# Layer-0 attention in bursts of six key tiles: maxima over two banks, the shift row put in by DMA, short units first, sums as products with a column of ones

## The chip, the cores and the metric

The kernel runs on one core of one Trainium2 chip, as one program. The metric is the device time of one execution in microseconds. Lower is better. The engines named below are PE (TensorE, matrix products; PEld is its weight load), DVE (VectorE), ACT (ScalarE), POOL (GpSimd) and SP (SyncE, which only issues DMAs here). They run at the same time, each through its own instructions in a fixed order, and wait for each other by semaphores.

## The reference

The reference is a two-layer backbone over 2048 latent tokens with a prefix of 256 context tokens, model width 1024, all in float32. Layer 0 runs a convolution branch beside grouped-query attention; layer 1 runs a Fourier branch beside neighbourhood attention. The change touches the attention of layer 0 alone. Cut to that:

```
ck = rms_norm(ck, kn_g)
q = axial_rope(rms_norm(q, qn_g))                 # 8 heads of 64
k = axial_rope(rms_norm(k, kn_g))                 # 2 key/value heads of 64
y_b = blocked_attn(q, concat([ck, k]), concat([cv, v]))   # 2304 keys
...
s = einsum('bqkgd,bskd->bkgqs', qg, k) * dh ** -0.5
p = softmax(s, axis=-1)
o = einsum('bkgqs,bskd->bqkgd', p, v)
...
yc_b = dense_attn(cq, ck, cv)                     # context queries: 256 keys
```

So 2048 latent queries of each of 8 heads see 2304 keys, and 256 context queries see the 256 context keys.

## The kernel before, in words

Tokens lie in 18 tiles of 128, the two context tiles first. A *unit* of the attention is 256 queries of two heads that share a key head: `(b, hp)`, with b the block of 256 tokens and hp the pair of heads. Its 4 x 128 = 512 query rows are the moving operand of the score products. A long unit (b from 1 to 8) goes over 18 key tiles, a short unit (b = 0, the context queries) over 2. There are 32 long and 4 short units; the short ones stand at places 0, 4, 8 and 12 of the list.

For each unit these functions run; all are closures in `ab_attention`:

- `load_q`, `load_high` (L866, L874): DMAs of the queries. A query is kept as a high and a low half in f32r; `q` holds both halves, `qm` the high half and further rows (see `shift_row`).
- `chunk` (L884, L886): maxima. The scores are computed once, roughly, with queries as stationary and 512 keys as moving operand into a PSUM bank of the pool `psm` (tile `m`, three buffers of one bank), and DVE reduces the bank to one column of `ast`. A long unit has 4 query tiles x 5 chunks, four of 512 keys and one of 256. The sign is turned, so the maximum is a minimum. `least` (L890) reduces the five columns to one.
- `shift_row` (L895, L896): the minima are transposed on PE into 4 rows, and DVE writes them, times a mask, into rows 64 to 67 of `qm`; the low half of the keys has four rows of ones there, so the second score product subtracts each query's shift.
- `score` (L907, L912): for one key tile two products into a bank of `pss` (tile `s`, two buffers), and ACT takes the exponential into `pr` (pool `apt`, six buffers).
- `multiply` (L922): for a pair of key tiles the value products, f32, 64 output columns each: the even tile into the upper half of the output partitions, the odd tile into the lower half, accumulated in one bank `av`. It stands three steps after the pair (LAG).
- `add` (L947): sums of the exponentials over key tiles; 11 of 18 tiles on POOL (`accp`), 7 on DVE (`accd`), two steps after the tile.
- `unload` (L930) copies `av` out on ACT. Then `join` (L952, POOL) adds the two sums, `sum_high` (L957, ACT) and `sum_low` (L962, DVE) split them into f32r halves, `total` (L972) multiplies a column of ones with both halves into one row, which ACT copies (L978) and a DMA spreads over 128 partitions (L980); `invert` (L986 to L989) takes the reciprocal, writes it to DRAM and reads it back broadcast to all partitions; `divide` (L993, POOL), `fold` (L998, L999, ACT) and `store` (L1005 to L1007) finish. The offsets of these eight are the tuple CHAIN.

The order of the work is written out by hand. A *step* is one key tile of one unit; `first[i]` is the step at which unit i starts. `at(step, order, f)` files a function under a step, and the loop at the end of `ab_attention` calls them by step and order, which fixes the order of instructions on PE, ACT, DVE and POOL (`manual_schedule`). Chunks of a unit are filed every 0.85 steps, the last of them 7 steps (AHEAD) before the unit's first score. SP's order isn't written out; the framework's scheduler places the DMAs. Beside the attention, `extra` runs side chains at given steps: adaLN products of the gate and of layer 1 (L238 and below), bias patterns for layer 1 (DMAs at L276 and near), and from step 220 on the first blocks of the layer's output stage.

## Time and profile before

| | us |
|---|---|
| three runs, lowest / median / highest | 2870.37 / 2875.66 / 2879.15 |
| the profiled execution, its own time | 2871.33 |
| its span, first to last instruction | 2869.4 |
| PE / weight loads busy | 2741.3 / 2107.3 |
| DVE / ACT / POOL busy | 1823.9 / 1117.7 / 1451.9 |
| value products `av`, PE busy | 315.5 |
| exponentials, ACT busy | 343.2 |
| first and last exponential of this attention, start | 705.1 and 1534.7 |

How to read it: times in the profile are microseconds from the start of the span, mean durations nanoseconds. A line of a group has the source line, the engine, the operation, the tiles as output<-input, the shapes, the number of instructions, and then the busy time with the mean of one, and the idle time of the engine just before them with what ended it. A line of the timeline has start, duration, engine, source line and the rest. Matmuls overlap: the end of one is modelled, and what one costs is the distance from its start to the start of the next. The granted clock is the share of TensorE's full clock.

### The profile page before, as it was taken

What the parts mean: (1) busy time and instruction counts of PE and PEld (TensorE: products, weight loads), DVE (VectorE), ACT (ScalarE), POOL (GpSimd) and SP (SyncE); (2) the same over time, 40 slices, a digit from 0 to 9 for tenths busy, and PEclk for the clock granted to TensorE, in tenths of its full rate; (3) what the DMA queues carried; (4) which work ended last, traced back from release to release, by engine and by line L of the source; (5) the groups of instructions that cost most, each with busy time, mean ns of one, the idle gap of its engine ahead of it and who ended that gap; (6) DMA issues with size and microseconds to landing.
All of it is one profiled execution on the core that took longest, in us unless ns stands there. A gap on an engine that the chain in (4) does not pass through costs nothing.

```text
span 2869.4 us, 41078 instructions
## 1 busy us (share of the span) xinstructions
PE 2741.3 (96%) x14481; PEld 2107.3 (73%) x14481; DVE 1823.9 (64%) x2867; ACT 1117.7 (39%) x2081; POOL 1451.9 (51%) x1223
## 2 busy tenths in 40 slices
PE   7998799999999999999999999999999998999898
PEld 5988799997444444444446787988898887888787
DVE  4798868888777888888886564111212336888563
ACT  3223130321455555555554233113222325888321
POOL 2658710720566787778885753122222312677342
PEclk9999899998999999999999999999999999999999
DMA  9546332475443433332123653433344339997862
GB/s 299 195 130 201 126 140 92 136 237 164 121 136 89 128 109 115 92 105 52 47 58 120 236 179 125 151 131 104 114 147 143 113 113 244 226 223 178 269 213 81
DMA packets 346232, 422.05 MB, mean 147 GB/s; under 512 B 56092, under 2 KB 266572, under 8 KB 341803
## 3 DMA queue, kind: packets, MB, share of 16 engines
q1 hardware_dynamic: 310315, 392.81, 45.2%
q10 hardware_dynamic: 35712, 26.62, 2.9%
q8 instruction: 114, 1.87, 0.3%
q14 instruction: 91, 0.75, 0.1%
HBM read 271.65 MB, written 152.84 MB: 148 GB/s over the span
## 4 chain that ended last, share of the span: by engine, by line
PE 67%; DMA 4%; DVE 3%; POOL 2%; issue 2%; ACT 1%; SPq 0%; POOLq 0%; ACTq 0%; DVEq 0%
PE av L922 9%; PE s L907 8%; PE mm L433 6%; PE m L884 6%; PE mm L431 6%; PE mm L432 6%; PE mo L1107 4%; PE mo L1108 4%; PE mo L1109 4%; PE npt L1670 3%; PE ns L1616 2%; PE nav L1691 1%; PE nav L1690 1%; PE mm L440 1%; PE mm L442 1%
## 5 line engine op out<-in xcount | busy, mean ns | idle before, releaser
L886 DVE TENSOR_REDUCE ast<-m 128x1 f32<-128x512 f32 (+1 forms) x656 | 398.2, 626 | 147.3 <-PE m L884 145.2
L912 ACT ACTIVATE pr<-s 128x512 f32<-128x512 f32 x584 | 343.2, 595 | 313.0 <-PE s L907 275.2
L947 POOL TENSOR_TENSOR accp<-accp,pr 128x512 f32<-128x512 f32 x283 | 399.4, 1411 | 87.1 <-ACT pr L912 72.5
L447 POOL TENSOR_TENSOR wlo<-wraw,whi 128x1024 fp32r<-128x1024 f32 x64 | 202.2, 3166 | 377.8 <-ACT whi L446 377.6
L533 DVE SCALAR_TENSOR_TENSOR acc<-u,cw,acc 128x1151 f32<-128x1151 f32 (+1 forms) x240 | 355.5, 1535 | 0.0
L922 PE MATMUL av<-pr,vt 128*64 128x512 f32 x1168 | 315.5, 619 | 0.0
L433 PE MATMUL mm<-hi_ab,wlo 128*128 128x384 f32 x768 | 259.0, 338 | 17.1 <-POOL wlo L447 15.6
L432 PE MATMUL mm<-lo_ab,whi 128*128 128x384 f32 x768 | 260.0, 339 | 0.0
L431 PE MATMUL mm<-hi_ab,whi 128*128 128x384 f32 x768 | 256.4, 340 | 3.0 <-ACT hi_ab L380 1.6
L431 PE MATMUL mm<-hi_cd,whi 128*128 128x512 f32 x640 | 250.8, 392 | 1.0 <-ACT hi_cd L380 1.0
L432 PE MATMUL mm<-lo_cd,whi 128*128 128x512 f32 x640 | 250.1, 391 | 0.4 <-DVE lo_cd L381 0.4
L433 PE MATMUL mm<-hi_cd,wlo 128*128 128x512 f32 x640 | 246.7, 390 | 0.0
L947 DVE TENSOR_TENSOR accd<-accd,pr 128x512 f32<-128x512 f32 x165 | 168.6, 1022 | 1.0 <-ACT pr L912 0.5
L884 PEld LDWEIGHTS m<-k1h,q 128*128 128x128 f32 x328 | 61.7, 188 | 132.8 <-DVE ast L886 87.1
L433 PEld LDWEIGHTS mm<-hi_ab,wlo 128*128 128x128 f32 x768 | 145.6, 190 | 18.1 <-POOL wlo L447 15.9
L884 PEld LDWEIGHTS m<-k0h,q 128*128 128x128 f32 x328 | 63.5, 196 | 125.1 <-DVE ast L886 80.2
L372 DVE TENSOR_SCALAR ht<-ptr,scale,shift 128x384 f32<-128x384 f32 (+2 forms) x96 | 61.1, 671 | 141.2 <-PE ptr L369 140.4
L431 PEld LDWEIGHTS mm<-hi_ab,whi 128*128 128x128 f32 x768 | 145.0, 190 | 5.0 <-ACT hi_ab L380 2.5
L1677 DVE TENSOR_TENSOR nlo<-npt,nhi 128x512 fp32r<-128x512 f32 x192 | 123.7, 645 | 38.7 <-ACT nhi L1675 37.4
L432 PEld LDWEIGHTS mm<-lo_ab,whi 128*128 128x128 f32 x768 | 145.6, 190 | 0.9 <-DVE lo_ab L381 0.8
L1639 POOL TENSOR_SCALAR npr<-npr,nst 128x640 f32<-128x640 f32 (+1 forms) x128 | 109.2, 861 | 67.9 <-DVE nst L1638 48.8
L431 PEld LDWEIGHTS mm<-hi_cd,whi 128*128 128x128 f32 x640 | 120.3, 188 | 26.0 <-ACT hi_cd L380 1.4
(322 smaller groups left out, 6934.4 us busy)
## 6 DMA issues: line engine op xcount, KB each, us to landing
wraw<-in_cd_w_in_dram SPq DMA_DIRECT2D x46, 512.0 KB, 3.8
pat_d<-big SPq DMA_DIRECT2D x72, 256.0 KB, 4.1
nv<-v_d SPq DMA_DIRECT2D x128, 128.0 KB, 6.7
adaraw<-in_ab_w_ada_dram SPq DMA_DIRECT2D x24, 512.0 KB, 8.2
adaraw<-in_cd_w_ada_dram SPq DMA_DIRECT2D x24, 512.0 KB, 3.6
nk<-k SPq DMA_DIRECT2D x20, 576.0 KB, 8.2
w_d<-whi SPq DMA_DIRECT2D x22, 512.0 KB, 2.8
w_d<-wlo SPq DMA_DIRECT2D x22, 512.0 KB, 4.8
```

The costliest lines, as they stand in the source:

```text
L431: nc.tensor.matmul(ps, a, hh[:, k, cols], start=k == 0, stop=False)
L432: nc.tensor.matmul(ps, a, hl[:, k, cols], start=False, stop=False)
L433: nc.tensor.matmul(ps, b, hh[:, k, cols], start=False, stop=k == KT - 1)
L447: (eng or nc.vector).tensor_tensor(out=lo, in0=src, in1=hi.bitcast(F32), op=ALU.subtract)
L533: ins = nc.vector.scalar_tensor_tensor(out=acc[:, :n], in0=u[:, tap : tap + n], scalar=cw[:, ch, tap : tap + 1], in1=acc[:, :n], op0=ALU.m ...
L884: nc.tensor.matmul(ps[:, :n], lhs, kt[hp // 2][0][:, a : a + n], start=True, stop=True)
L886: nc.vector.tensor_reduce(out=s["st"][:, qt, col : col + 1], in_=ps[:, :n], axis=AX.X, op=ALU.min)
L907: nc.tensor.matmul(ps[:], kt[hp // 2][key][:, k * P : k * P + P], s[x][:].rearrange("p j n -> p (j n)"), start=key == 0, stop=key == 1,)
L912: nc.scalar.activation(pr[:], ps[:], AF.Exp, scale=-1.0)
L922: nc.tensor.matmul(s["av"][x * 64 : x * 64 + 64], vt[:, k - 1 + x, kv * 64 : kv * 64 + 64], s["pr"][k - 1 + x][:], start=k == 1, stop=k == ...
L947: eng.tensor_tensor(out=s[name][:], in0=first_in[:], in1=s["pr"][k][:], op=ALU.add)
L1677: return lambda: nc.vector.tensor_tensor(out=lo[:, :o], in0=pt[:, :o], in1=hi[:, :o].bitcast(F32), op=ALU.subtract)
```

## The change

1. `units`: the four short units come first, then the 32 long ones. The chunks of the short units are filed at steps -4 to -1, those of the first long unit at steps 0 to 7, of the second at 9 to 19, of the others every 2 steps (RATE).
2. `chunk`: 1024 elements at a time, over two banks: two products of 512 keys of one query tile, reduced by one instruction; the last 256 keys of all four query tiles make the ninth chunk. The pool `psm` has two buffers of two banks, and the bank of `psr` goes.
3. `shift_row`: no transpose. DVE negates the minima into a column tile `sr`, and four DMAs on SP put each of its columns as a row of 128 values into row 64 of `qm`. The keys' low half has one row of ones, so the second score product has 65 rows instead of 68.
4. `multiply`: six key tiles at a time (GROUP), in the step of the last of the six, after that step's chunk.
5. `add`: DVE takes tiles 4, 5, 10, 11, 15, 16, 17, filed at the end of their burst; POOL the others, one step after the tile. Short units have no addition.
6. `total`: no join, no split, no row copy. For each of the four query tiles `accp` and `accd` are stationary operands in f32 and a column of ones is the moving one; the result is a column in a tile of `psm`; DVE takes the reciprocal, one DMA writes it to DRAM, one reads it broadcast. For the last unit a 128x128 matrix of ones is stationary and the sums move.
7. `unload` is filed one step after the unit's end instead of three, and the offsets of what follows change; some pools have other sizes; the adaLN parts begin at step 4 instead of -8, and the DMA of their bias is issued a stage later.

```diff
-            ps_m = self.pool(es, "psm", 3, PSUM)
+            ps_m = self.pool(es, "psm", 2, PSUM)
...
-            ps_r = self.pool(es, "psr", 1, PSUM)
...
-            AHEAD, LAG, SUM, RATE, ROW = 7, 3, 2, 0.85, 4
+            AHEAD, SUM, RATE, GROUP = 7, 1, 2, 6
...
-            for hp in range(4):
-                units.insert(4 * hp, (0, hp))
+            units = [(0, hp) for hp in range(4)]
+            units += [(b, hp) for kv in range(2) for b in range(1, 9) for hp in (2 * kv, 2 * kv + 1)]
...
+                ps = ps_m.tile([P, 1024], F32, name="m", tag="m")
+                key = kt[hp // 2][0]
+                if b and c < 8:
+                    parts = [(c // 2, c % 2 * 1024 + x * 512, 512) for x in range(2)]
+                else:
+                    parts = [(qt, 2048 if b else 0, 256) for qt in range(4)]
+                for x, (qt, a, n) in enumerate(parts):
+                    lhs = s["q"][:, qt // 2, (qt % 2) * P : (qt % 2) * P + P]
+                    nc.tensor.matmul(ps[:, x * n : x * n + n], lhs, key[:, a : a + n], start=True, stop=True)
+                if len(parts) == 2:
+                    nc.vector.tensor_reduce(
+                        out=s["st"][:, c // 2, c % 2 : c % 2 + 1], in_=ps[:], axis=AX.X, op=ALU.min
+                    )
...
             def shift_row(i):
                 s = state[i]
-                pt = ps_r.tile([P, 512], F32, name="row", tag="row")
-                nc.tensor.transpose(pt[0:4, 0:P], s["st"][:, :, 5], self.ident[:])
-                nc.vector.scalar_tensor_tensor(
...
+                row = sp.tile([P, 4], F32R, name="sr", tag="sr")
+                nc.vector.tensor_scalar(out=row[:], in0=st[:, :, 3], scalar1=-1.0, scalar2=None, op0=ALU.mult)
+                for qt in range(4):
+                    to = s["qm"][64:65, qt // 2, (qt % 2) * P : (qt % 2) * P + P].bitcast(F32)
+                    nc.sync.dma_start(to.rearrange("o (n f) -> o n f", f=1), row[:, qt : qt + 1].bitcast(F32))
...
-            def multiply(i, k):
+            def multiply(i, first_k, n):
...
-                for x in range(2):
+                for k in range(first_k, first_k + n):
+                    x = k % 2
...
+            def by_dve(i):
+                return [4, 5, 10, 11, 15, 16, 17] if i < len(units) - 1 else list(range(TAIL, NT))
...
+                for f in range(4):
+                    for x in ("accp", "accd"):
+                        nc.tensor.matmul(
+                            pt[:, f : f + 1], s[x][:, f * P : f * P + P], self.ones[:, 0:1], start=x == "accp", stop=x == "accd"
+                        )
+                rc = sp.tile([P, 4], F32, name="rc", tag="rc")
+                nc.vector.reciprocal(rc[:], pt[:, 0:4])
+                inv = self.inv_d[i % 4]
+                nc.sync.dma_start(inv.rearrange("o (f p) -> (o p) f", p=P), rc[:])
...
+                if i < 4:
+                    when = [i - 4]
+                elif i == 4:
+                    when = [max(x - 1, 0) for x in range(9)]
+                elif i == 5:
+                    when = [9 + x * 5 // 4 for x in range(9)]
+                else:
+                    when = [first[i] - AHEAD - RATE * (8 - x) for x in range(9)]
...
+                at(when[-1], 5.5, bind(shift_row, i))
...
-                    if k % 2 == 1:
-                        at(s + LAG + 0, 3, bind(multiply, i, k))
-                    at(s + SUM, 6, bind(add, i, k))
+                    end = min(k // GROUP * GROUP + GROUP, n)
+                    if k == end - 1:
+                        at(s, 5, bind(multiply, i, k // GROUP * GROUP, end - k // GROUP * GROUP))
+                    late = k in by_dve(i) and i < len(units) - 1
+                    at(first[i] + end - 1 if late else s + SUM, 6, bind(add, i, k))
                 e = first[i] + n - 1
-                at(e + LAG, 4, bind(unload, i))
...
+                at(e + 1, 9, bind(unload, i))
+                if i < 4:
+                    ds = (3, 10, 15, 16)
+                elif i < len(units) - 1:
+                    ds = (8, 15, 18, 19)
+                else:
+                    ds = (2, 3, 4, 5)
+                for d, f in zip(ds, (total, divide, fold, store)):
+                    at(e + d, 3 if f is total else 9, bind(f, i))
```

More of the change, by code (lines that the diff above doesn't have):

```diff
@@ L959, in sum_low @@
[L959 to L964 removed]
             def total(i):
                 s = state[i]
[L969 to L973 removed]
+                pt = ps_m.tile([P, 1024], F32, name="m", tag="m")
@@ L974, in total @@
+                if i == len(units) - 1:
+                    for x in ("accp", "accd"):
+                        nc.tensor.matmul(pt[:, 0:512], self.ones[:], s[x][:], start=x == "accp", stop=x == "accd")
                     s["r"] = rp.tile([P, 512], F32, name="r", tag="r")
-                    nc.vector.reciprocal(s["r"][:], pt[:])
+                    nc.vector.reciprocal(s["r"][:], pt[:, 0:512])
                     return
-                row = rp.tile([1, 512], F32, name="srow", tag="srow")
```

130 lines of the change are left out of this document (41 added, 89 removed).

## The prediction

> **What bounds the kernel now.** I read the head of the page first, then the table of stretches around the attention of layer 0, then the groups of that stretch with shapes kept apart.
>
> ```profile
> span 2869.4 us, 41078 instructions
> ```
> ```profile
> 685.00:706.30 21.30, 16.86 (x41) 9.53 (x40) 17.16 (x34) 2.75 (x4) 0.00 (x0) 0.60 0.99 310
> 706.30:1536.40 830.10, 811.80 (x3392) 384.16 (x3390) 674.19 (x1028) 445.19 (x800) 616.80 (x474) 1.00 0.33 95
> ```
> ```profile
> L912 ACT ACTIVATE pr<-s 128x512 f32<-128x512 f32 x584 | 343.2, 595 | 313.0 <-PE s L907 275.2 <-DVE ast L886 13.5 <-POOL accp L947 10.8
> L886 DVE TENSOR_REDUCE ast<-m 128x1 f32<-128x512 f32 x512 | 342.6, 685 | 112.7 <-PE m L884 110.8
> L922 PE MATMUL av<-pr,vt 128*64 128x512 f32 x1168 | 315.5, 619 | 0.0
> L886 DVE TENSOR_REDUCE ast<-m 128x1 f32<-128x256 f32 x144 | 59.9, 418 | 34.6 <-PE m L884 34.4
> ```
>
> The columns of a stretch are its length, the busy time of PE, weight loads, DVE, ACT and POOL, then the granted clock. From the first score of the first long unit (706.3, see the start below) to the end of the last value product, PE is busy for 811.8 of 830.1 us at full clock; DVE for 81%, POOL 74%, ACT 54%. ACT waits 275 us for scores, DVE 111 us for chunks: PE is the bound. So only PE's order of work counts, and a busy PE hides the waste that its order makes. I therefore work with start-to-start times of matmuls.
>
> ```profile
> 1000.87 0.39 PE L972 MATMUL row<-sh,onesr 128*1 128x512 f32 x1
> 1001.09 0.39 PE L972 MATMUL row<-sl,onesr 128*1 128x512 f32 x1
> 1001.32 0.39 PE L907 MATMUL s<-q,k0h 128*128 128x512 f32 x1
> ...
> 1002.13 0.39 PE L907 MATMUL s<-qm,k0l 68*128 68x512 f32 x1
> 1002.45 1.08 PE L922 MATMUL av<-pr,vt 128*64 128x512 f32 x4
> 1003.46 0.50 PE L884 MATMUL m<-k0h,q 128*128 128x512 f32 x1
> 1003.80 0.39 PE L907 MATMUL s<-q,k0h 128*128 128x512 f32 x1
> 1004.03 0.40 PE L907 MATMUL s<-qm,k0l 68*128 68x512 f32 x1
> ```
>
> A full-width pass of 512 columns starts 0.23 us before the next (1003.80 to 1004.03). The two value products of a pair (four records, since an f32 product is two passes) take 1.01 (1002.45 to 1003.46). They also enter late, 0.32 after the last score instead of 0.23, and leave late, 0.34 instead of 0.23. A pair so costs 1.01 + 0.09 + 0.11 = 1.21 us.
>
> **The change, part by part.** *Bursts of six.* At the end of the last unit two pairs already stand together:
>
> ```profile
> 1534.56 1.94 PE L922 MATMUL av<-pr,vt 128*64 128x512 f32 x8
> 1536.42 0.61 PE L1143 MATMUL pl<-mean_w,sm 128*128 128x1 f32 x4
> ```
>
> Four tiles take 1.86, so the second pair adds only 0.85. A burst of six is 1.01 + 2 x 0.85 + 0.20 = 2.91 against 3 x 1.21 = 3.63: 0.72 less. The 32 long units have three bursts each: 96 x 0.72 = **-69 us**. The exponentials of the burst's last tiles are in time: its third pair starts 1.7 us into it.
>
> *Sums by a column of ones.* `total` now issues 8 products with a 128x128 f32 stationary operand and one moving column. L1143, two products in code and four records, has this form:
>
> ```profile
> 1302.84 0.65 PEld L1143 LDWEIGHTS pc<-mean_w,sm 128*128 128x128 f32 x4
> 1303.41 0.19 PEld L907 LDWEIGHTS s<-q,k1h 128*128 128x128 f32 x1
> ```
> ```profile
> 1006.41 0.27 PE L895 MATMUL row<-ident,ast 128*4 128x128 f32 x1
> 1006.44 0.48 PE L907 MATMUL s<-q,k0h 128*128 128x512 f32 x1
> ```
>
> Four loads take 0.57 to the next line's load; the first stands behind a 0.23 pass, so each further one costs (0.57 - 0.23) / 3 = 0.113. Sixteen cost about 15 x 0.113 = 1.70 us per unit. What goes is L972, 0.45 (1000.87 to 1001.32), and the transpose L895, 0.03. Net 1.22 x 32 = **+39 us** (the last unit sums with full-width products instead; I charge it the same). [...]
>
> Also gone is the wait of L972 for its low half; join, split and row copy go from POOL, ACT and DVE, which do not bound.
>
> ```profile
> PE row L972 <- DVE sl L962: 8.3, 6, 2.5
> POOL o L993 <- DMA r<-inv: 77.7, 33, 4.1
> ```
>
> **-8 us**. The POOL wait for the inverse shrinks too (divide comes 8 steps after the sum instead of 5 after the inversion) but POOL has room, so nothing.
>
> *Two-bank maxima.* The reductions cost 0.685 for 512 and 0.418 for 256, a slope of 0.267 per 256, hence 1.22 for 1024; 9 x 1.22 = 11.0 per unit replace 16 x 0.685 + 4 x 0.418 = 12.6. DVE gains, PE's passes stay the same in number. A chunk comes every second step, about 1.4 us apart, so two buffers do; if DVE were late by its three gathered adds (about 3 us) the burst of 2.9 us covers it. Zero.
>
> *Scores in rows of six.* Only two score banks remain between PE and ACT, and six scores now follow each other without a value product among them.
>
> ```profile
> 1004.53 1.24 ACT L912 ACTIVATE pr<-s 128x512 f32<-128x512 f32 x2 [1.31 <-PE s L907]
> ...
> 1014.22 0.60 ACT L930 ACTIVATE o<-av 128x512 f32<-128x512 f32 x1 [0.42 <-PE av L922]
> 1014.84 0.42 ACT L998 ACTIVATE yb<-o 64x256 f32<-64x256 f32 x1
> ...
> 1015.72 1.08 ACT L912 ACTIVATE pr<-s 128x512 f32<-128x512 f32 x2
> ```
> ```profile
> 803.98 1.07 ACT L912 ACTIVATE pr<-s 128x512 f32<-128x512 f32 x2
> ...
> 804.61 0.19 PEld L907 LDWEIGHTS s<-q,k0h 128*128 128x128 f32 x1 [0.46 <-ACT pr L912]
> ```
>
> The exponential starts 0.50 after its second pass (1004.03 to 1004.53); PE may use the bank again 0.63 after that (803.98 to 804.61). With 0.23 between passes a bank turns in 1.36. PE needs 2 x 0.46 + 0.46 for two scores and a chunk, 1.38: it just fits. But `unload` (0.60, queued exponentials being 1.08 - 0.60 = 0.48 apart) now stands one step after a unit's end, ahead of the second exponential of the next row, where 0.02 is the slack. It pushes a score by about 0.5: 32 x 0.5 = **+16 us** (bounds: 0 if the delay is absorbed, +19 at 0.60). The fold (two of 0.42) lies in the burst. The rest of ACT's work here is that of the side chains, five small groups of which the largest is
>
> ```profile
> L1163 ACT ACTIVATE sq<-cv,lg 128x256 f32<-128x256 f32 x12 | 6.8, 590 | 1.7 <-DVE cv L1158 1.7
> ```
>
> Under 30 us in all, it falls on rows (where it stops PE) or on bursts (where it does not), and partly waits anyway: **+8** (0 to +30).
>
> *The row by DMA.* Each unit issues four transfers of 128 x 4 bytes on SP, after the last chunk. Nearest rows:
>
> ```profile
> r<-inv SPq DMA_DIRECT2D x35, 256.0 KB, 4.1
> ...
> rc<-srow SPq DMA_DIRECT2D x35, 2.0 KB, 2.0
> ```
> ```profile
> L980 SPq DMA_DIRECT2D rc<-srow x35: 476/506/528, 721.3 to 1527.5; - x35
> ```
> ```profile
> L986 DVE RECIPROCAL rc<-rc 128x4 f32<-128x4 f32 x35 | 5.9, 168 | 0.3
> ```
> ```profile
> SPq L980 <- ACT pr L912: 212.6, 34, 12.0
> SPq L1007 <- POOL yb L1006: 129.9, 32, 10.0
> ```
>
> Reduction 1.22, two small operations on 4 columns (0.17 each, like L986), four issues of 0.51, landing 2.0 to 4.1: 5.6 to 7.7 us. The chunk stands at step 11 of the unit before; until the first score lie a burst, a row of 6 x 0.46 + 3 x 0.46 = 4.1, and a burst: 9.9. So it is hidden with 2 to 4 us to spare. If it lay behind SP's waits for POOL (130/32 = 4.1 us on average) some would miss: **+4** (0 to +96, the rival below). [...]
>
> *Short units first.*
>
> ```profile
> 685.62 1.09 DVE L886 TENSOR_REDUCE ast<-m 128x1 f32<-128x256 f32 x3 [3.89 <-PE m L884]
> 690.10 0.23 DVE L844 CAST onesr<-ones 128x128 fp32r<-128x128 f32 x1 [3.39 <-issue]
> ```
> ```profile
> 705.10 0.60 ACT L912 ACTIVATE pr<-s 128x512 f32<-128x512 f32 x1 [17.39 <-PE s L907]
> ```
> ```profile
> 706.29 0.40 PE L907 MATMUL s<-q,k0h 128*128 128x512 f32 x1
> ```
>
> Today DVE sets the start: 685.6 to 706.3, 20.7 us, with one short unit inside. The three others cost PE 1.21 + 4 x 0.23 + 4 x 0.12 + 0.48 = 3.1 each later, 9.3. Then all four lie in the start, which becomes 13 reductions (15.9) and two exposed rows (unit 0's and unit 4's, which is due one step after its last chunk, about 4.5 each less 3 x 1.22 of overlap): some 21 to 26 us, less the pause of 3.4 before `onesr` if it goes with that tile. **-4 us** (-12 to +5).
>
> Sum: -69 + 39 - 8 + 16 + 8 + 4 - 4 = **-14 us**. The profiled execution took 2871.3, its span and 1.9 outside it; the median of the runs shown is 4.3 above it. Against the median: **2861 us**.
>
> **The rivals.** *The rows come late (slower).* From 9.9 us after its last chunk every further microsecond stops PE at the unit's first score, with all that is queued behind. If SP's order puts a row behind a wait like that for POOL (4.1) or ACT (212.6 / 34 = 6.3), it misses by 2 to 4 us: 32 x 3 = +96, in place of the 4: 2953. It decides the sign from 0.8 us per unit. For it speak those two waits; against it that the store lies eleven steps before the row in the order of work, and that L980, the wait of 6.3, is removed. 0.12.
>
> *ACT paces the rows (no change).* The slack of 0.02 per turn is as small as the error of these rows; if each of 96 rows loses a further 0.2, -14 + 19 = +5: 2881. For it speaks the turn of 1.36; against it that the sum's 1.7 us gives ACT time in one row of three. 0.22.
>
> *The rows of six run clean (faster).* No stall by unload or other ACT work, the start as short as its bound: -69 + 39 - 8 - 12 = -50: 2826. For it speaks that ACT is only 54% busy; against it that its order is fixed. 0.16.
>
> *Products of one column are cheap.* If the loads of the sum's sixteen products all hid behind each other, the sum would cost what L972 cost, the 39 falls out and -14 becomes -53: 2823. The L1143 rows speak against it. [...] 0.03.
>
> **How the numbers follow.** The forecast has the remaining 0.47, with its own range from 2849 to 2875. About 0.3% (8.6 us) is what a measurement of this kernel can tell from no change. Of the forecast's chance 0.36 lies beyond that as faster, 0.11 within; with the clean and the cheap case faster has 0.55. The ACT case is split, 0.14 same and 0.08 slower; with the late rows slower has 0.20, same 0.25. The range from 2823 to 2897 holds all but the late rows and the ends.
>
> **What would show it.** Bursts: twelve records of `av` in about 2.7 us, 0.43 between pair starts. Sums: sixteen records of `total` 0.11 apart, 1.7 us per unit. Unload: a PE wait for `pr` near 0.5 at the fourth score of a unit. Rows: no PE wait for the row's DMA beyond the start. Wrong would be: bursts over 3.1 us, PE idle at each unit's first score, a reduction of 1024 well over 1.22, or a period per long unit other than about 25 us (now 830.1 with 3 short units in it, some 25.6 for each of 32).

## The result, and the profile after

The changed kernel takes 3014.95 us (median; 3010.80 to 3018.06) beside 2873.01 us (2869.08 to 2879.15) for the kernel before, timed together: a ratio of 1.049, 95% interval 1.047 to 1.051. The forecast was 2861. The whole of the loss lies in the attention of layer 0. From its first score to its last value product the kernel before took 832.5 us (704.0 to 1536.5 of its span). The head of the page after, and the stretch of the same work, with the columns of the prediction's table of stretches:

```profile
span 3008.6 us, 41671 instructions
```
```profile
694.90:1669.90 975.00, 889.82 (x3858) 514.62 (x3857) 563.43 (x641) 392.96 (x725) 542.10 (x438) 0.90 0.33 85
```

975 us, 142 more. Two things are new against before: PE is busy for only 890 of the 975, and its granted clock is 0.90 where it was 1.00. The groups of instructions on the other hand are what was forecast:

```profile
L916 ACT ACTIVATE pr<-s 128x512 f32<-128x512 f32 x584 | 333.6, 597 | 475.5 <-PE s L911 464.6 <-POOL accp L955 3.9 <-DVE accd L955 3.2
L887 DVE TENSOR_REDUCE ast<-m 128x1 f32<-128x1024 f32 x256 | 311.9, 1223 | 213.9 <-PE m L885 213.5
L928 PE MATMUL av<-pr,vt 128*64 128x512 f32 x1168 | 279.5, 612 | 0.0
```

A reduction of 1024 takes 1.22 us, and the value products' busy time fell from 315.5 to 279.5. But in these groups ACT and DVE now wait for PE 1.7 and 1.9 times as long as before (464.6 us against 275.2, and 213.5 against 110.8). So PE is late, not slow at the new work. Its timeline over a burst and a sum, in matmul records:

```profile
1102.49 2.79 PE L928 MATMUL av<-pr,vt 128*64 128x512 f32 x12
1105.21 0.50 PE L911 MATMUL s<-q,k0h 128*128 128x512 f32 x1
...
1115.43 0.28 PE L969 MATMUL m<-ones,accp 128*128 128x1 f32 x2
...
1116.91 0.36 PE L969 MATMUL m<-ones,accd 128*128 128x1 f32 x2
1117.13 0.70 PE L885 MATMUL m<-k0h,q 128*128 128x512 f32 x2
...
1118.25 0.63 PE L911 MATMUL s<-q,k0h 128*128 128x512 f32 x1
1118.67 0.63 PE L911 MATMUL s<-qm,k0l 65*128 65x512 f32 x1
```

A burst of six lasts 2.72 us (1102.49 to 1105.21) and a sum 1.70 us (1115.43 to 1117.13). Behind the sum something unforeseen begins: a score pass (one product of 512 columns) takes 0.42 us (1118.25 to 1118.67) where 0.23 is normal. The table of stretches around it, the granted clock third from the end, shows why:

```profile
1114.58:1117.99 3.41, 3.41 (x24) 3.10 (x24) 0.30 (x2) 1.09 (x2) 2.10 (x2) 1.00 0.00 0
1117.99:1121.41 3.42, 3.42 (x10) 2.68 (x9) 2.32 (x2) 1.49 (x3) 3.26 (x4) 0.50 0.07 1
1121.41:1124.82 3.41, 3.41 (x18) 1.30 (x16) 2.43 (x6) 0.90 (x2) 1.65 (x2) 1.00 0.00 0
```

For 3.41 us the clock is half, though PE was busy for all of the 3.41 us ahead. Half clock adds up to 198 us in this stage, the attention of layer 0; before, it was 5 us. Not all of it has this origin. From the end of the first long unit on there are 32 such stretches. Ahead of 19 of them PE is busy throughout and 13 or 16 one-column records of a sum lie in the 3.41 us, as above. Ahead of the other 13 there is no such record, and PE stands still for a third of the 3.41 us or more, as here:

```profile
1131.64:1135.06 3.42, 1.78 (x9) 0.61 (x6) 2.86 (x3) 0.83 (x2) 3.35 (x4) 1.00 0.38 109
1135.06:1138.47 3.41, 3.41 (x10) 2.66 (x9) 2.00 (x3) 2.17 (x4) 2.24 (x2) 0.50 0.62 161
```

So half clock also follows 3.41 us in which PE waits. The second new thing is in the waits (total us, times, longest):

```profile
SPq L977 <- DMA inv<-rc: 285.4, 35, 10.5
```
```profile
ACT yb L986 <- POOL o L981: 101.6, 27, 10.6
POOL o L981 <- DMA r<-inv: 98.1, 31, 17.1
...
PE s L911 <- DMA qm<-sr: 51.1, 17, 16.7
```
```profile
r<-inv SPq DMA_DIRECT2D x35, 256.0 KB, 5.8
qm<-sr SPq DMA_DIRECT2D x144, 0.5 KB, 4.0
inv<-rc SPq DMA_DIRECT2D x35, 2.0 KB, 8.4
```

Writing the inverse sums to DRAM (`inv<-rc`) now takes 8.4 us from issue to landing; it took 2.0 with the same 2 KB before. The column of sums holds query f x 128 + p on partition p, so the write is 512 pieces of 4 bytes, where it was 128 of 16. SP stands behind it 285 us in all, the read back is issued late, POOL's divide waits for it, and the fold waits on ACT for the divide, with the next unit's exponentials queued behind the fold.

### The profile page after: what moved, and what is told of

It reads as the page before. It is cut to its first block, busy times and chain, and to the rows that moved or that the text cites. A ratio compares the mean times of both kernels' runs of the same rounds, so it can differ in the third digit from the quotient of the medians.

```text
span 3008.6 us, 41671 instructions
## 1 busy us (share of the span) xinstructions
PE 2811.1 (93%) x14937; PEld 2233.5 (74%) x14937; DVE 1707.0 (57%) x2462; ACT 1069.2 (36%) x2010; POOL 1375.4 (46%) x1191
## 4 chain that ended last, share of the span: by engine, by line
PE 59%; DMA 10%; issue 3%; POOL 3%; DVE 2%; ACT 2%; SPq 1%; POOLq 0%; ACTq 0%; DVEq 0%
PE s L911 8%; PE av L928 6%; PE mm L432 6%; PE mm L434 6%; PE mm L433 6%; PE m L885 4%; DMA inv<-rc 3%; PE mo L1103 3%; PE mo L1104 3%; PE mo L1105 3%; PE npt L1666 2%; PE m L969 2%; PE ns L1612 1%; DMA qm<-sr 1%; PE nav L1687 1%
## 5 line engine op out<-in xcount | busy, mean ns | idle before, releaser
L916 ACT ACTIVATE pr<-s 128x512 f32<-128x512 f32 x584 | 333.6, 597 | 475.5 <-PE s L911 464.6
L955 POOL TENSOR_TENSOR accp<-accp,pr 128x512 f32<-128x512 f32 x283 | 377.9, 1335 | 241.0 <-ACT pr L916 229.7
L887 DVE TENSOR_REDUCE ast<-m 128x1 f32<-128x1024 f32 x256 | 311.9, 1223 | 213.9 <-PE m L885 213.5
L928 PE MATMUL av<-pr,vt 128*64 128x512 f32 x1168 | 279.5, 612 | 0.0
L928 PEld LDWEIGHTS av<-pr,vt 128*64 128x64 f32 x1168 | 76.9, 139 | 144.4 <-issue 138.1
L911 PE MATMUL s<-qm,k0l 65*128 65x512 f32 x292 | 128.3, 439 | 37.8 <-DMA qm<-sr 32.6
L911 PE MATMUL s<-q,k1h 128*128 128x512 f32 x292 | 141.5, 485 | 17.6 <-ACT pr L916 17.6
L955 DVE TENSOR_TENSOR accd<-accd,pr 128x512 f32<-128x512 f32 x165 | 140.1, 849 | 17.6 <-ACT pr L916 5.8
L911 PE MATMUL s<-qm,k1l 65*128 65x512 f32 x292 | 130.0, 445 | 20.5 <-DMA qm<-sr 18.5
L911 PE MATMUL s<-q,k0h 128*128 128x512 f32 x292 | 140.0, 479 | 8.6 <-ACT pr L916 8.5
```

The lines of the kernel that those rows point to most:

```text
L887: nc.vector.tensor_reduce(out=s["st"][:, c // 2, c % 2 : c % 2 + 1], in_=ps[:], axis=AX.X, op=ALU.min)
L911: nc.tensor.matmul(ps[:], kt[hp // 2][key][:, k * P : k * P + P], s[x][:].rearrange("p j n -> p (j n)"), start=key == 0, stop=key == 1,)
L916: nc.scalar.activation(pr[:], ps[:], AF.Exp, scale=-1.0)
L928: nc.tensor.matmul(s["av"][x * 64 : x * 64 + 64], vt[:, k, kv * 64 : kv * 64 + 64], s["pr"][k][:], start=k < 2, stop=k >= tiles[i] - 2,)
L955: eng.tensor_tensor(out=s[name][:], in0=first_in[:], in1=s["pr"][k][:], op=ALU.add)
```

## The experiments

Two theories stood at the start. *Waits*: the bursts' gain is lost where the inverse, and what queues behind it, comes late. *Products and clock*: it is lost to the thin one-column products and the half clock behind them. A third, that the bursts themselves gain nothing, was kept as rival throughout.

To place the time I cut PE's order into bursts and rows: a row runs from the first matmul behind a burst to the next burst's first record, so each long unit has rows 0, 1 and 2, row 0 with the unload and the fold of older units in it and row 1 with the sum. Summed over 32 units, the rows of the kernel after take 284, 239 and 163 us, of which 105, 68 and 6 us are at half clock; its undisturbed row 2 is 4.57 us.

**e1: the inverse in 16-byte pieces.** The stationary operands take every fourth query, so that a partition holds four neighbours:

```diff
-    pt[:, f : f + 1], s[x][:, f * P : f * P + P], self.ones[:, 0:1], start=x == "accp", stop=x == "accd"
+    pt[:, f : f + 1], s[x][:].rearrange("p (n f) -> p f n", f=4)[:, f], self.ones[:, 0:1], start=x == "accp", stop=x == "accd"
-    nc.sync.dma_start(inv.rearrange("o (f p) -> (o p) f", p=P), rc[:])
+    nc.sync.dma_start(inv.rearrange("o (p f) -> (o p) f", f=4), rc[:])
```

> The changed kernel, but the stationary slice of each sum product takes every fourth query, so the reciprocals go to DRAM as 128 pieces of 16 bytes instead of 512 of 4. Theory A (the 4-byte write of the inverse takes 8.4 us, SP stands behind it for 285 us, and rows and inverses come late): the write lands in about 2 us, the PE wait for the row (53 us) and the POOL wait for the inverse (98 us) nearly vanish, time falls by 80 to 140 us to 2875 to 2935. Theory B (the one-column products let the granted clock fall to half): the write is faster but the 17 half-clock stretches right behind the sums stay, time falls by 20 us or less from this alone. Both together: about 2915, with some 60 to 90 us at half clock left of 198.

Measured 2997.82 us, ratio 1.0438 (1.0411 to 1.0465).

```profile
inv<-rc SPq DMA_DIRECT2D x35, 2.0 KB, 1.4
```
```profile
ACT yb L986 <- POOL o L981: 24.1, 23, 6.2
```

The write lands in 1.4 us, the fold's wait falls from 101.6 to 24.1, and row 0 falls from 284 to 189 us: that chain of waits was as described. But the strided load doubled the sum (16 records 0.23 us apart take 3.66 us from the first start to the last end, against 1.84 so counted before), and now row 1 runs into half clock in 31 units of 32 (239 to 317 us). The time fell by 17 us, within theory B's bound and far from theory A's 80 to 140, but that is chance: one loss was swapped for the other.

**e2: full-width products of ones for all units.**

```diff
-    if i == len(units) - 1:
+    if True:
```

> The changed kernel, but every unit sums as its last one does: a 128x128 matrix of ones stationary, the sums moving (512 columns), reciprocal from PSUM on DVE, no DMA of the inverse at all. PE time per sum is about the same 1.7 us (four f32 passes of 0.43). Theory A: rows in time, time falls to 2870 to 2900 and nothing more is explained by the clock. Theory B: no half clock behind the sums, since 512 columns stream. A and B together: the prediction's terms hold, 2850 to 2875, half clock under 20 us outside the start. Theory C (ACT's order paces the rows of six): PE still waits for pr, 60 us or more, time 2880 to 2910.

Measured 3015.56 us, ratio 1.0493 (1.0458 to 1.0527).

```profile
PE m L885 <- DVE r L965: 71.6, 33, 6.7
```

No inverse goes through DRAM, and row 0 is 203 us. But a reciprocal of 128x512 takes DVE 3.36 us, it holds a buffer of maxima for that time, and PE waits for it: row 1 is 299 us. Every range was missed. Row 1 has half clock in 20 units although no one-column product is left in them: ahead of each stretch PE is busy for at most 51% of the 3.41 us.

**e3: the rows put in through PE again**, as in the kernel before (transpose, masked copy, four rows of ones):

```diff
-    row = sp.tile([P, 4], F32R, name="sr", tag="sr")
...
+    nc.tensor.transpose(pt[0:4, 0:P], st[:, :, 3], self.ident[:])
+    nc.vector.scalar_tensor_tensor(
+        out=s["qm"][64:68].rearrange("p j (i n) -> p (j i) n", n=P),
...
```

> The changed kernel, but the shift row is made on PE and DVE as before (transpose into a psm tile, masked write into four rows of qm), so no row DMA. Sums and inverse stay as changed. Theory D (the row DMAs themselves are what costs): time falls by 100 us or more, to 2870 to 2915. Theory A: only the 53 us of row waits go, the inverse still lands in 8 us and POOL and ACT still wait for it: 2950 to 2980. Theory B: half clock behind the sums stays as it is.

Measured 3024.74 us, ratio 1.0527 (1.0492 to 1.0561): no better. With no row transfer left, the fold and the divide wait longer than before:

```profile
POOL o L983 <- DMA r<-inv: 141.9, 33, 18.9
...
ACT yb L988 <- POOL o L983: 121.7, 25, 12.7
```

So the row's DMAs are not the main cost, and theory D falls. Theory A's range, 2950 to 2980, was missed as well: the row waits went, and longer waits for the inverse took their place.

**e4: the kernel before with bursts of six alone.** Maxima, rows, sums and their cadence of 0.85 steps stay.

```diff
-    if k % 2 == 1:
-        at(s + LAG + 0, 3, bind(multiply, i, k))
+    if k == end - 1:
+        at(s, 5, bind(multiply, i, k // 6 * 6, end - k // 6 * 6))
```

> The kernel before, with only the value products gathered into bursts of six in the step of the last tile (eight pr buffers, unload one step after the unit's end, the row of sums written into a free part of accd so that the memory fits). The prediction's first term: 96 x 0.72 = 69 us less on PE, so 2804 if nothing else; with the stalls of rows of six on ACT (16 + 8) 2828. Rival C (ACT paces rows of six): most of the 69 is lost to PE waits for pr: 2855 to 2880.

Measured 2995.86 us, ratio 1.0428 (1.0396 to 1.0460).

```profile
PE row L973 <- DVE sl L963: 50.7, 28, 5.6
...
PE m L884 <- DVE ast L886: 37.4, 51, 2.3
```

The bursts last 2.73 us here too, but one-bank maxima every 0.85 steps and the sum now meet rows without value products, and PE waits for DVE; the stage has 116 us of half clock, none of it behind 3.41 us in which PE was busy throughout. Both ranges were missed. Bursts alone lose; whether the cadence of the maxima or the place of the sum would have to change with them was not taken apart.

**e5: the read of the inverse issued from ACT's queue, nine steps after the sum**, with divide, fold and store later:

```diff
-    nc.sync.dma_start(s["r"][:], inv[:].broadcast_to((P, 512)))
+    nc.scalar.dma_start(s["r"][:], self.inv_d[i % 4][:].broadcast_to((P, 512)))
```

> The changed kernel, but the broadcast read of the inverse is its own step, 9 steps after the sum, issued from ACT's queue; divide, fold and store follow 7 steps later than before. SP so never stands behind the 8.4 us write, and the stationary slices stay contiguous (the strided ones of the earlier run cost 3.66 us per sum instead of 1.84). Theory A (SP behind the inverse): row waits of 53 us and the waits of POOL (98) and ACT (102) go; the first row of a unit falls from 6.4 (10.0 at half clock) to about 5.0 us, time falls by 100 to 125 us to 2890 to 2915. Theory B (half clock behind the sums): second rows stay at 6.3 clean and 7.8 with half clock, 60 us or more of half clock stay, and the time stays above 2880. If A is all, half clock nearly vanishes with the waits and the time is 2850 to 2870.

Measured 2988.62 us, ratio 1.0388 (1.0353 to 1.0423), far above the 2890 to 2915 of theory A. Row 0 has a median of 5.05 us in the 22 units where it has no half clock, but ACT itself stands at the read where the write is late (9.3 us, 6 times), exponentials behind it, and single bursts then last up to 10.4 us. Row 1 keeps its half clock in 13 units.

**e6: the long units' sums made as before** (join on POOL, two halves, two products with a column of ones stationary and 512 sums moving), the rest as in the kernel after:

```diff
+    fs = (join, sum_high, sum_low, total_row, invert, divide, fold, store)
+    ds = (2, 6, 6.5, 8, 12, 17, 18, 19)
```

> The changed kernel, but long units sum as before: join on POOL, split into high and low half, two products of a column of ones with 512 moving columns, row copied out, spread and written back in 16-byte pieces. So the 1.84 us of one-column products and the 8.4 us write are both gone; bursts, two-bank maxima, row DMAs and the order of units stay. Theories A and B together: rows of a unit take 5.0, 5.0 to 5.5 and 4.6 us and a burst 2.73, a unit about 23 us against 25.6 now, half clock under 40 us in all (the start), time 2790 to 2830. Theory C (ACT's order paces the rows): rows stay over 5.5 us, time 2850 to 2880.

Measured 2971.96 us, ratio 1.0333 (1.0296 to 1.0371), where 2790 to 2830 or, by theory C, 2850 to 2880 was expected. Row 1 falls to 170 us and has no half clock in any of 32 units. Row 0 stays at 303 us:

```profile
ACT yb L1022 <- POOL o L1017: 138.7, 30, 6.2
...
POOL o L1017 <- DMA r<-inv: 72.0, 24, 11.0
```

The sum now takes four steps longer to reach the inverse. The divide is filed only two steps later (17 for 15) and the fold at its old place, so both are late again. So the fold's place is a cause of its own beside the write.

**e7: e5 with a join on POOL first, so that a sum is 8 records instead of 16.**

```diff
-    for x in ("accp", "accd"):
+    for x in ("accp", "accd") if i < 4 else ("accd",):
```

> As the kernel with the inverse read on ACT's queue, but POOL adds the two partial sums first, so a unit has 4 one-column products instead of 8: 0.9 us instead of 1.84. Against that kernel: PE alone gives 0.9 x 32 = 29 us. Theory B says more, since half the thin stretch should no longer drop the clock: half clock behind the sums in few units, 50 to 90 us less in all. If the clock does not depend on the sums: about 29 us less.

Measured 2992.03 us, ratio 1.0396 (1.0368 to 1.0424), no gain on e5 where 29 us or more was expected, since ACT's read disturbs more bursts (23 over 3 us for 17, up to 10.3 us). But half clock in row 1 came in 4 units where e5 had 13. In two of the 4 it begins ahead of the sum, in the other two PE was busy for only 0.58 and 0.78 of the 3.41 us ahead, so none of it is behind the sum alone. With e6 (none in row 1) and e1 (31 of 32 at 3.66 us) that is a dose in these runs: the longer the thin products last, the more units have half clock in row 1.

**e8, e9 and e10.** e8 is e6, sums included, with the divide, fold and store later (20, 24 and 25 steps after the unit's end), and with the short units' read of the inverse filed apart from its write (the second line: sum, read, divide, fold, store):

```diff
+    ds = (2, 6, 6.5, 8, 12, 20, 24, 25)
...
+    ds = (3, 12 + 2 * i, 15 + 2 * i, 17 + 2 * i, 18 + 2 * i)
```

> Edit: the kernel after, with the long units' sums made as before (three adds of slabs, the chain of four on DVE, one product of the row of ones by accd, which is 1 record where the one-column products are 16), and with the read of the inverse, the divide, the fold and the store filed later (20, 24 and 25 steps for a long unit in place of 17, 18 and 19 in the last run), and for the short units the read of the inverse filed apart from its write, so that SP stands behind no write. Waits theory (what the bursts gain is lost where PE waits for exponentials that stand behind a fold on ACT, which waits for the divide, which waits for the inverse): row 0 falls from 7.24 and 9.14 us to about 5.0, row 1 and row 2 stay at 5.0 and 4.5, the start loses its stall of some 17 us for the first long unit's row. 11 x 2.2 + 21 x 4.1 = 110 us, plus 15 to 20 at the start, less than the last run's 2964 us span: 2835 to 2850 us, and the half clock nearly gone from the stage: faster than before (2871). Rival (the bursts of six themselves leave PE waiting, whatever the sums and the fold do): row 0 stays above 6.5 us with PE waiting for the exponentials, and the time stays above 2930.

The expectation describes the sums as another form; the edit has those of e6, a join on POOL, two halves and two products of 512 columns.

e9 moves the short units' reads in the same way and the long units' read, divide, fold and store to steps 17, 22, 24 and 25, but keeps the one-column sums and their 4-byte write:

> Edit: the kernel after, with its sums by one-column products kept, and only the read of the inverse filed apart from its write and later (17 steps), the divide, fold and store behind it (22, 24 and 25 steps), and so for the short units too. It differs from the run beside it in the sums of the long units alone. Clock theory (thin products of 1.84 us in all set off stretches of half clock of 3.41 us): the sums cost 1.84 - 0.48 = 1.36 us each, 44 us over 32 units, and in a third to a half of the units row 1 is about 1.5 us longer for the lower clock (13 to 19 units, 20 to 30 us): 50 to 75 us above the run beside it, at 2885 to 2925. Rival (the half clock comes from PE's idle time alone, and goes with the waits): only the 44 us, with the half clock of the stage under 60 us in all and row 1 at 6.3 us in nearly all units. Second rival (the one-column sums cost nothing that the adds on POOL and DVE did not cost): no difference above 10 us.

e10 is e8 with `GROUP = 2`:

> Edit: the kernel of the first of these runs, with the value products in bursts of two key tiles in place of six; everything else as there. If a burst of six saves what the profile of before gave as 0.72 us in six tiles (three bursts of 1.15 us, 3.45, against one of 2.73), the time is 96 x 0.72 = 69 us above that run, or 50 to 69 with part of it lying beside waits of PE. Rival (the bursts of six hold up the scores behind them and so give their gain back): within 15 us of that run, or below it.

e8: 2867.44 us, ratio 0.9987 (0.9970 to 1.0004), no difference that can be told from before. The waits theory had this gain right in kind (105 us below e6) and was 17 us short of its range. To compare the steady state I take the last 20 long units, from the end of the twelfth to the end of the last, in the table of stretches with the value products' line alone (720 records; length, PE and weight loads busy, clock, DMA share, GB/s). The kernel before, after, e8 and e10:

```profile
1038.20:1536.50 498.30, 194.67 (x720) 35.90 (x720) 1.00 0.26 76
```
```profile
1105.30:1669.90 564.60, 169.80 (x720) 46.89 (x720) 0.91 0.26 68
```
```profile
1053.90:1521.50 467.60, 167.72 (x720) 46.34 (x720) 1.00 0.30 83
```
```profile
1107.70:1669.80 562.10, 255.43 (x720) 65.12 (x720) 1.00 0.24 68
```

Per long unit: 24.9 before, 28.2 after, 23.4 in e8, 28.1 in e10. The bursts do gain once the waits are gone; what e8 lacks lies in its first units. e10 (3021.82 us, ratio 1.0517, 1.0491 to 1.0544; 154 us above e8 where 50 to 69 was expected) refuted its own rival but not cleanly: its pairs stand in the step of their second tile, so PE waits at each for that exponential, and the value products' busy time is 12.8 us a unit where the pairs of before have 9.7. e9 (3095.26 us, ratio 1.0785, 1.0749 to 1.0820) missed all its expectations:

```profile
SPq L982 <- DMA inv<-rc: 285.4, 32, 11.1
```
```profile
PE s L911 <- DMA qm<-sr: 124.6, 25, 18.8
```

SP's wait for the 4-byte write was not removed, only moved to where the next unit's row stands behind it. It shows what such a wait is worth in the wrong place, and prices nothing else.

**e11: e8 with its start changed.** In e8 the first long unit's row stood behind two 4-byte writes of short units, and PE waited 17 us. Here that unit's maxima go two to a step, and the short units' writes, filed apart from their sums (second entry of the second tuple), come behind its row:

```diff
-    when = [max(x - 1, 0) for x in range(9)]
+    when = [-1, 0, 0, 1, 1, 2, 2, 3, 4]
...
-    ds = (3, 12 + 2 * i, 15 + 2 * i, 17 + 2 * i, 18 + 2 * i)
+    ds = (3, 5, 13 + 2 * i, 16 + 2 * i, 17 + 2 * i, 18 + 2 * i)
```

> Edit: the kernel of the run e8 (bursts of six, row sums, late divide and fold), with the start alone changed: the first long unit's maxima two to a step (its row leaves SP about 8 us earlier), and the short units' inverse writes in 4-byte pieces filed two steps behind their reciprocals, so behind that row on SP. Waits theory (what e8 lacked against its steady 23.3 us per long unit, where the kernel before has 24.9, lies at the start: PE stood 18 us for the first long unit's row, behind two inverse writes): the first long unit ends 20 to 27 us earlier than in e8 (771 us into the span there, 744 in the kernel before), and the time falls from 2867 to 2840 to 2850: faster than before by about 1%. Rival (what e8 lacks at its start is the half clock and the maxima's reduces on DVE, not the row): within 8 us of e8.

2860.83 us beside 2875.32 for the kernel before: ratio 0.995 (0.9934 to 0.9967), faster than both kernels, than the one before by 0.5%. The stall at the start, of after and of e11:

```profile
734.94 0.77 PE L911 MATMUL s<-qm,k0l 65*128 65x512 f32 x1 [16.73 <-DMA qm<-sr]
```
```profile
721.08 0.76 PE L913 MATMUL s<-qm,k0l 65*128 65x512 f32 x1 [4.42 <-DMA qm<-sr]
```

The gain on e8 is 7 us, not 20 to 27: PE had the row 16 us earlier (721.1 against 736.9 in e8), but the first long unit ended only 6 us earlier (765.0 against 771.4), with 22 us of half clock in between. The time lies in the rival's bound, within 8 us of e8; which of the rival's two causes holds the start back, half clock or DVE's reductions, is open.

**e12: e11 with one-column sums, and the 128x4 of sums turned on PE**, so that the inverse leaves in four pieces of 512 bytes:

```diff
+    nc.tensor.transpose(pt[0:4, 512 : 512 + P], s["cs"][:], self.ident[:])
+    nc.vector.reciprocal(s["rc"][:], pt[0:4, 512 : 512 + P])
...
+    nc.sync.dma_start(inv.rearrange("o (f p) -> (o f) p", p=P), s["rc"][:])
```

> Edit: the run e11, with the long units' sums made by the kernel after's one-column products (16 records, 1.84 us; no joining add on POOL, no halves on ACT and DVE), and the 128x4 of sums turned by one product on PE, so that the inverse goes to DRAM in four pieces of 512 bytes and no 4-byte piece is left in the long units. It prices the products and the clock apart from the write. Clock theory (the thin products set off half clock for 3.41 us): 44 us for the products themselves (32 x (1.84 - 0.48)) and 13 to 19 units with row 1 about 1.5 us longer: 60 to 75 us above e11, with the half clock's time 45 to 65 us more. Rival (the half clock came with the waits for the 4-byte writes): 35 to 50 us above e11, with row 1 at 6.3 us and no more half clock than in e11. Second rival (POOL's joining add and the halves on ACT and DVE cost as much as the products): within 15 us of e11.

2942.85 us, ratio 1.0239 (1.0219 to 1.0259): 82 us above e11, 7 beyond the clock theory's range and far from both rivals'. Rows 0 and 2 are those of e11 (186 and 167 against 187 and 166 us); row 1 grows from 176 to 250 and the bursts from 265 to 275, with half clock in row 1 in 18 units of 32 and in none of e11's. The last 20 units of e11 and of e12:

```profile
1043.80:1510.30 466.50, 167.76 (x722) 46.34 (x720) 1.00 0.30 83
```
```profile
1078.10:1595.90 517.80, 174.09 (x720) 48.02 (x720) 0.94 0.25 75
```

So the one-column sums cost about twice what their records were estimated to take (82 us for 44), with no long unit's wait behind a 4-byte write.

What decides which units are hit? The traces record when the granted clock changes, and here it is 1.00 or 0.50. The 24 records of the kernel before and the 94 of the kernel after begin within 5 ns of a grid of 3.4133 us in each trace, the shortest stretch of half clock is 3.413 us, and in e12 too every such stretch begins on this grid. I call one stretch of the grid a window. Two sums of e12, by windows (clock third from the end):

```profile
1112.71:1116.12 3.41, 3.41 (x25) 2.79 (x23) 1.04 (x2) 2.20 (x4) 2.55 (x2) 1.00 0.52 151
1116.12:1119.53 3.41, 3.13 (x9) 2.43 (x9) 2.42 (x3) 1.42 (x3) 2.54 (x2) 0.50 0.16 44
1119.53:1122.95 3.42, 3.42 (x12) 1.35 (x13) 2.42 (x5) 0.60 (x1) 0.00 (x0) 0.50 0.91 313
1061.49:1064.90 3.41, 3.41 (x25) 3.04 (x24) 0.70 (x2) 1.10 (x3) 2.45 (x3) 1.00 0.11 38
1064.90:1068.32 3.42, 3.14 (x16) 2.02 (x17) 3.23 (x4) 2.24 (x4) 2.67 (x3) 1.00 0.03 8
```

Both sums lie at the start of their window (at 1112.80 and 1061.92) with PE busy throughout. The first was followed by half clock, the second not, so the place in the window alone does not decide. Over all units half clock mostly goes with it. Counted from its first record to the start of the next product, a sum that lies inside one window was followed by half clock in 11 of 17 (after: 18 of 19), one split about evenly over two in 0 of 6 (after: 0 of 2). The expectation of e13 counts slightly otherwise, 11 of 15 and 16 of 17.

The traces allow a count that covers PE's waits as well: the moving columns of all matmul records that start in a window, 512 to a pass. Most windows have 10 passes or more (before 219 of 231, after 160 of 260). Over the kernels before and after and all fourteen runs, from the end of the first long unit to the last value product (in the kernel before and e4, whose order is another, from the same number of value products), a window at full clock with fewer than 5 passes was followed by half clock in 103 of 106, one with 5 to 8 in 156 of 242, one with 8 or more in 4 of 3273; in the kernel after alone in 6 of 6, 26 of 35 and 0 of 176. A window with all sixteen records of a sum in it has 5 to 8 passes (after and e12), although PE is busy nearly all the time.

**e13 and e14.** e13 issues e12's products in two groups of eight, six steps apart:

```diff
-    for f in range(4):
+    for f in (2 * half, 2 * half + 1):
...
+    fs = (total_row, total_rest, turn, invert, divide, fold, store)
+    ds = (8, 14, 15, 17, 23, 26, 27)
```

> Edit: the run e12 with the sixteen records of a long unit's one-column products issued in two groups of eight, six steps (about 7 us) apart, with the inverse, divide, fold and store filed 3 to 5 steps later; the same products in the same number. In e12 and in the kernel after, every stretch of half clock starts on a grid of 3.413 us, and a sum whose 1.84 us lie inside one grid window is followed by a window at half clock (11 of 15 in e12, 16 of 17 in the kernel after), while a sum that straddles two windows about evenly (0.7 to 1.1 us in each) is not (0 of 6 in e12). Window theory: groups of 0.92 us never fill that much of a window, so row 1 loses its half clock (64 us of it in e12, worth about 26 us of time) and the products' own 44 us stay: 2905 to 2925, and the half clock in rows 1 and 2 under 15 us. Rival (any one-column products, in what dose ever, drop the clock): two drops per unit in place of one, 2943 to 2990. Second rival (the drop follows the sum's waits and not its products): no change, 2935 to 2950.

2911.06 us, ratio 1.0133 (1.0104 to 1.0162), inside the window theory's range and 32 us below e12 with the same products. The last 20 units:

```profile
1071.80:1568.20 496.40, 167.73 (x722) 46.33 (x720) 1.00 0.28 83
```

The clock is back at 1.00. From the end of the first long unit on there is no half clock at all, in row 1 or in row 2, where the second group now lies; e12 has 85 us there. Both rivals fall: twice as many groups did not drop the clock more often, and in e12 PE was busy for at least 92% of the window ahead of each half-clock stretch, so its waits were not the cause.

e14 undoes the bursts in e11, with pairs three steps behind their tile as in the kernel before:

```diff
-    AHEAD, SUM, RATE, GROUP = 7, 1, 2, 6
+    AHEAD, SUM, RATE, GROUP = 7, 1, 2, 2
...
-    at(s, 5, bind(multiply, i, k // GROUP * GROUP, end - k // GROUP * GROUP))
+    at(s + 3, 3, bind(multiply, i, k // GROUP * GROUP, end - k // GROUP * GROUP))
...
-    at(e + 1, 9, bind(unload, i))
+    at(e + 3, 4, bind(unload, i))
```

> Edit: the run e11 with the value products in pairs, each three steps behind its tile as in the kernel before (the run e10 had its pairs in the step of their second tile, where PE stood for that tile's exponential: 12.8 us of value products per long unit against 9.7 in the kernel before and 8.4 in e11), and the unload two steps later. Burst theory (a burst of six saves 0.72 us, or 0.90 by the measured 2.73 us against three pairs of 1.21, and pairs hide the unload's 0.5 us per unit): 96 x 0.9 = 86 less 16, so 55 to 75 us above e11, at 2915 to 2935. Rival (the bursts are worth nothing, since rows of six wait for ACT what the bursts save): within 15 us of e11.

2931.15 us, ratio 1.0206 (1.0180 to 1.0231): 70 us above e11, inside the burst theory's range. The last 20 units, and the largest wait of PE in the whole attention:

```profile
1075.00:1591.60 516.60, 198.00 (x720) 35.78 (x720) 0.98 0.28 75
```
```profile
PE m L979 <- DVE sl L971: 39.5, 30, 2.3
```

The value products' busy time alone is 198.0 against 167.8 over 20 units, 1.5 us a unit, 48 over 32. The wait for the sum's low half, 39.5 us, was 5 in e11, so the 70 holds up to 34 us that the edit brought with it: undoing the bursts costs between 36 and 70. That the range was met is partly luck: its 0.90 sets the records of a burst (2.73) against whole pairs with their late entry and exit (1.21).

## Why the prediction was wrong, point by point

The distance from before to after is +142 us. By the medians of the runs it splits into -14 (before to e11: everything but the sums), +82 (e11 to e12: one-column sums, of which 26 to 32 are the clock, e12 to e13) and +72 (e12 to after: the 4-byte write and all that queues behind it, with the earlier places of divide and fold and the stall at the start, not taken apart); the 2 us left over are the kernel before, which was measured anew beside each run. The clock has a part in the +72 too: the stage has 198 us of half clock in the kernel after and 125 in e12.

*Bursts of six, -69: right.* The records of a burst take 2.73 us; it enters and leaves 0.10 us late each, as a pair does, so a burst costs 2.93 where 2.91 was worked out. Against three pairs of 1.21 that saves 0.70, or 67 us. By e14 it is 36 to 70 net of what comes with it.

*Unload, +16: right.* In e11, where row 0 has neither sum nor stall, its median is 5.01 us against 4.58 for row 2: 0.43 a unit, 14 us.

*Sums, +39: the mechanism right, the term mis-sized.* The records came as forecast, 1.70 us a sum. In e13 the one-column sums cost 50 us above e11, 11 more than forecast (the turn and PE's waits for maxima are in it). With the clock they cost 82 (e12). That the granted clock differs with PE's order (over the last 20 units 0.94 in e12, 1.00 in e13 with the same products) had no place in the sum: I read it as a constant, because it was 1.00 over the whole stage of before.

*"The POOL wait for the inverse shrinks too ... but POOL has room, so nothing": the step that failed.* I counted steps between sum and divide (7 by the offsets 8 and 15, not 8) and put no duration on the write of the inverse, though its access pattern had changed to 4-byte pieces; the row of before with its 2.0 us was at hand. It became 8.4, and with 5.8 for the read back that is 14.2 us, where 7 steps are about 10 (25.6 us for 18). POOL's wait did not shrink, it rose from 77.7 to 98.1 us. That POOL has room was true and beside the point: the divide's successor, the fold, stands on ACT ahead of the next unit's exponentials. I had noted that the fold lies in a burst and did not ask what it waits for. For the row's transfers of 128 x 4 bytes I did estimate a landing, from 2.0 to 4.1 us, and missed that the inverse write has 4-byte pieces too. For the row e3 shows no gain from doing without it; the write took 8.4 us in 4-byte pieces and 1.4 in 16-byte ones (e1).

*The row by DMA, +4, and the rival "the rows come late".* The transfer itself was sized right (landing 4.0, between 2.0 and 4.1; issue 0.59 for 0.51), and e3 shows that the rows are not the main loss. The rival had the right kind, SP's order putting rows behind a wait, but the wrong wait: not POOL's store or ACT, but SP's own read of the inverse behind its write. Its price of 96 us stood for a stall in every unit; PE's waits for rows came to 51 us in 17 places.

*Wait for L972's low half, -8.* It is gone with its products. In e11, with row sums, it is 5 us, so nothing in it speaks for one-column sums.

*Two-bank maxima, 0.* The reduction of 1024 is 1.22 us as forecast, and PE waits for maxima 3 us in all of e11. In e4, with bursts and the old maxima, PE waits 37 us for them, so they may be what makes room for the bursts; they were not undone alone.

*Short units first, -4: wrong in sign.* By the trace's 52nd value record (equal numbers of value products done), the kernel before is at 744.4 us, after at 777.3, e11 at 765.0. So the start costs 33 us, 21 with the row's wait shortened. From there to the last value product before takes 792.1 us and e11 745.3: a gain of 47, part of it given back by the start and by 10 us more behind the attention (1342.5 against 1332.9 us to the end of the span). Which part of the start is the order of units, which the half clock and which the exposed row was not taken apart.

*The other ACT work, +8*, was not told apart. The rivals of ACT's pace and of clean rows concerned tens of microseconds of a balance that two larger terms settled. That one-column products are cheap is refuted by the 0.11 us between records.

The range and the chances rested on a sum in which neither the write nor the clock had a term, and no rival stood for either.

That e11, which keeps the bursts and drops the one-column sums, lands at 2861 like the forecast is no support for the forecast's sum: it lacks the +39 and pays the start instead.

## What to carry to other kernels

When an operation's output changes its layout, follow it through the DMA that stores it: the same 2 KB landed here in 8.4 us as 512 pieces and in 1.4 as 128 (e1), and SP stood 285 us in all behind the slow write. For each late result ask what its consumer's consumer stands ahead of: POOL, with room, held up PE through ACT's fixed order (ACT waited 101.6 us for the divide). And on PE, look for the price of thin products in their records and in the granted clock behind them: here 82 us (e12), of which 26 to 32 were the clock. Split in two groups they cost 50 (e13), and with the long operand moving row 1 had no half clock at all (e6). In these traces the columns that moved in a window told more of the next window's clock than the share of time for which PE is shown busy: with fewer than 5 passes half clock came next in 103 of 106, with 8 or more in 4 of 3273, while ahead of 19 of the 32 stretches of the kernel after PE was busy for the whole 3.41 us.

## What the runs showed of the hardware

- The granted clock halved with no PE idle (after, 1114.58 to 1121.41): PE busy for 3.41 of 3.41 us, 1.7 of them in one-column products, and the next 3.41 us ran at 0.50. With half the products in a group it did not happen behind any sum (e13). The stretches begin on a grid of 3.4133 us (within 5 ns, before and after). Half clock followed such sums, and it followed windows in which PE stood still for a third of the time or more (13 stretches of the kernel after). What sets the clock is not shown. Moving columns went with it (fewer than 5 passes of 512: half clock next in 103 of 106 windows; 8 or more: in 4 of 3273), but 6 of 17 sums that lay inside one window in e12 had no half clock behind them.
- Half clock cost less than its length says: 85 us of it in e12, none in e13 (from the end of the first long unit on), went with 32 us of time by the medians and 26 by the two profiled executions.
- A DMA of 2 KB into DRAM: 8.4 us to land as 512 pieces of 4 bytes, 2.0 and 1.4 us as 128 pieces of 16 (before, e1).
- An f32 stationary operand with a stride of four elements: 0.23 us between one-column records, against 0.11 with neighbouring elements (e1).
- A reciprocal of 128x512 takes DVE 3.36 us (e2).
